# A bidirectional RWKV-7 time-mixing stage on one core: two interleaved chains become one, and the 64-row output products become 128-row products

## The chip, the core and the metric

The kernel runs on one core of a Trainium2 chip. The time is the device time of one execution in microseconds (us). The engines are TensorE (PE: matmuls and transposes), VectorE (DVE), ScalarE (ACT), GpSimd (POOL) and SyncE (SP, which here only issues DMAs). TensorE's results land in PSUM, 8 banks of 128 partitions by 512 floats; everything else on the chip lies in SBUF, 128 partitions wide.

## The reference

One layer over 2048 latent tokens and 256 context tokens, width 1024, all in float32: a modulated norm and one input projection feed two groups of heads (neighbourhood attention and RWKV-7 time mixing, 8 heads of 64 each), then come an output projection, a gated residual and a SwiGLU feed-forward block. The change lies in the time mixing, which runs a recurrence over a 64x64 state per head, once forward and once backward:

```python
def wkv_scan(s0, r, w, k, v, a, b, reverse):
    # S <- S diag(w) + (S a) b^T + v k^T ;  y = S r
    def step(s, inp):
        r_t, w_t, k_t, v_t, a_t, b_t = inp
        sa = jnp.einsum('bhvk,bhk->bhv', s, a_t)
        s = s * w_t[:, :, None, :] + sa[..., None] * b_t[:, :, None, :] + v_t[..., None] * k_t[:, :, None, :]
        return s, jnp.einsum('bhvk,bhk->bhv', s, r_t)
    ...
# per direction: the 256 context tokens from a zero state, then the 2048 latent tokens;
# y of both directions is summed, group-normed, a bonus added, multiplied by a gate g
mix = jnp.concatenate([o_na, o_rw], axis=-1) @ w_out
h = h + mod[2][:, None, :] * mix
h = h + mod[5][:, None, :] * swiglu(modulate(rms_norm(h, norm2_g), mod[3], mod[4]), ffn_w_in, ffn_w_out)
```

## The kernel before

There are three stretches. **Phase 1** (to about 900 us) makes the modulation, the norm and the input projection, and writes the operands of attention and time mixing to DRAM. **Phase 2** (about 900 to 1988 us) runs attention and time mixing together. **Phase 4** (from 1988 us) makes the output projection, the residual and the feed-forward block.

In phase 2 the recurrence is cut into 36 chunks of 64 tokens, numbered m = 2s + c (s from 0 to 17, c 0 or 1); both directions of a chunk are worked at once. The context takes s = 0 and 1, which give no output, so 32 chunks have outputs. Five kinds of work are prepared per chunk or per pair of s: `builds` (L1002: products of the decayed keys and queries, masked into `ga` and `gb` by DVE at L1014 and into `lx` by ACT at L1008), `inverses` (L1053 to L1113: the inverse of a triangular 64x64 block by 32x32 products, for both s of a pair), `lates` (L1035: transposes that give `tt`), and the loads of values into `zv` (`load_v`, L1126). The `ga` and `gb` live in a ring of NU = 17 units, in which unit (4s + head pair + SHIFT) mod NU is used.

The **chain** carries the state z from chunk to chunk. It runs as two streams, `chains(0)` and `chains(1)`, each with four of the eight heads (two pairs q, the two heads of a pair lying in partitions 0 to 63 and 64 to 127) and both directions dd. Per chunk and stream it is: copy z into the free half of `zv` (L1175 ACT, L1176 DVE); a batch of 8 products (L1180), copied by ACT to `rs` (L1184); a batch of 8 (L1188), copied back into `zv` by ACT and DVE (L1172); a batch of 8 (L1195), added to z by DVE (L1200); the output products, z by `ga` over 64 rows (L1206) and `zv` by `gb` over 128 rows (L1209), summed in PSUM; a multiplication of z by the chunk's decay (DVE, L1212); two ACT copies of the output (L1216) and four stores (`store_y`, L1134). Each float32 product shows as two MATMUL records in the trace, a transpose as one.

Who comes first is set by `emit` (L862): every stream of work yields what it will use and how long by a table, and the stream that could start earliest, shifted by its entry in `LATE`, is written next. The tile framework then orders instructions again by its own estimates while it resolves waits and buffers; `Run` and `issue_after` keep a batch in one piece in that second ordering. In phase 4 `TimeMixOutput` (TMO, L1239 to L1283) turns one tile of 128 tokens of y into the normed, gated mix: it loads `gup`, `lng` and `lnb` once (L1252) and `mx`, `y`, `v`, `gd` per tile (L1262 to L1265), multiplies by the gate's weights on PE (L1267), and runs some 14 operations on POOL, DVE and ACT, which form one chain for a tile. `prepared` transposes the mix on PE (L1404), and L1446 multiplies it by `w_out`; the first half of its sum is over attention, the second over time mixing. Phase 4's tiles reuse the SBUF of phase 2, so they wait for whatever lay at the same addresses.

Of the kernel before, what the change touches and what calls it, by code (L numbers as in the profile page):

```python
# [93 lines left out]
def phase1(k):  # L94

    tc, nc, I = k.tc, k.nc, k.I
    with ExitStack() as ctx:
# [295 lines left out]
        def work_build(ops, hp, t0):  # L393
# [4 lines left out]
            for dd in range(2):  # L398
# [19 lines left out]
                nc.gpsimd.tensor_copy(k.pc[:, s0:s0 + 2, hp // 2, :, 2 * dd + hp % 2],  # L418
# [428 lines left out]
NU = 17  # L847
# [10 lines left out]
LATE = (60, 60, 60, -10, -10, 0, 0, 0, 60, 0)  # L858
# [53 lines left out]
def phase2(k):  # L912
# [4 lines left out]
    with ExitStack() as ctx:  # L917
# [9 lines left out]
        pch = [ps[6 + g].tile([P, 2, 4, 64], F32, name=f"pch{g}") for g in range(2)]  # L927
# [43 lines left out]
        def build(s, hp, w):  # L971
# [164 lines left out]
        def chains(g):  # L1136

            z = ch.tile([P, 2, 2, 64], F32, tag=f"z{g}", name="z0", bufs=2)
            nc.gpsimd.memset(z, 0.0)
            if g:  # L1140
                load_v(0)
                yield "post", ("values", 0)
            yield "run", ("DMA", 2.2)
            for s in range(NS):
                yield "wait", ("inv", s // 2, 2 * g + 1)
                us = [U.pop((s, 2 * g + q)) for q in range(2)]
                for c in range(2):
                    m = 2 * s + c
                    yield "wait", ("values", m), ("late", m, g)
                    if g and m + 1 < 2 * NS:  # L1150
                        load_v(m + 1)
                        yield "post", ("values", m + 1)
# [4 lines left out]
        dq = [(dd, q) for dd in range(2) for q in range(2)]  # L1157
        kept = []

        def chain(s, c, g, z, us):  # L1160
            lx, j0 = LX[s // 2], 4 * (s % 2)
            zv = ZV[2 * s + c]
            tt = TT_.pop((2 * s + c, g))
            rp, up_ = pch[g][:, 0], pch[g][:, 1]
            gs = slice(P * g, P * g + P)

            def slot(h, dd, q):
                return zv[:, h, dd, P * g + 64 * q:P * g + 64 * q + 64]

            def keep():  # L1170
                for h, copy in ((0, nc.scalar.copy), (1, nc.vector.tensor_copy)):
                    copy(zv[H[h], h, :, gs], up_[H[h]].rearrange("p (d q) n -> p d (q n)", d=2))  # L1172

            yield "run", ("ACT", 0.27), ("DVE", 0.2)
            nc.scalar.activation(zv[H[0], 0, :, gs], z[H[0]].rearrange("p d q n -> p d (q n)"), AF.Copy)  # L1175
            nc.vector.tensor_copy(zv[H[1], 1, :, gs], z[H[1]].rearrange("p d q n -> p d (q n)"))  # L1176
            yield "run", ("PE", 0.57)
            for i, (dd, q) in enumerate(dq):
                for h in range(2):
                    nc.tensor.matmul(rp[H[h], i, :], us[q].ga[:, h, 2 * dd + c, :], slot(h, dd, q),  # L1180
                                     start=True, stop=True)
            yield "run", ("ACT", 0.27)
            rs = ch.tile([P, 4, 64], F32, tag=f"rs{g}", name="rs")
            nc.scalar.activation(rs, rp, AF.Copy)  # L1184
            yield "run", ("PE", 0.57)
            for i, (dd, q) in enumerate(dq):
                for h in range(2):
                    nc.tensor.matmul(up_[H[h], i, :], lx[H[h], 2 * g + q, j0 + 2 * dd + c, :], rs[H[h], i, :],  # L1188
                                     start=True, stop=True)
            yield "run", ("ACT", 0.27), ("DVE", 0.33)  # L1190
            keep()
            yield "run", ("PE", 0.57)
            for i, (dd, q) in enumerate(dq):
                for h in range(2):
                    nc.tensor.matmul(rp[H[h], i, :], tt[:, q, dd, H[h]], slot(h, dd, q),  # L1195
                                     start=True, stop=True)
            yield "run", ("DVE", 0.34)
            z2 = ch.tile([P, 2, 2, 64], F32, tag=f"z{g}", name="z2", bufs=2)
# [12 lines left out]
            yield "run", ("DVE", 0.34)  # L1211
# [484 lines left out]
```

## Time and profile before

| | |
|---|---|
| median of 3 runs | 3618.38 us (3614.16 to 3624.52) |
| the profiled execution | 3615.05 us, span 3613.3 us |
| mean granted TensorE clock | 0.944 of full speed |
| PE busy | 3433.7 us, 95% of the span |
| DVE, ACT, POOL busy | 68%, 43%, 29% |

A share of busy time is an average over phases with different limits; the stretches in the rows below are read one by one. The granted clock has two levels, 1.2 and 2.4 GHz; a stretch's value is the mean over it.

### The profile page before, as it was taken

How to read it: one execution, taken by the hardware profiler on the slowest of the kernel's cores; microseconds unless marked ns; L12 is line 12 of the kernel's file. 1: busy time of each engine (PE TensorE's matmuls, PEld its weight loads, DVE VectorE, ACT ScalarE, POOL GpSimd, SP SyncE). 2: the span in 40 equal slices, each digit the busy share in tenths (PEclk: the TensorE clock that was granted, in tenths of full speed). 3: DMA queues.
4: the chain of work that ended last, by engine and by line, in shares of the span. 5: the costliest groups of instructions: out<-in, count | busy, mean ns of one | idle time of the engine just before them, and what ended most of it. 6: DMA issues, size and time to landing. Idle time of an engine off the chain costs nothing. (4 is left out here: it accounts for less than half of the span.)

```text
span 3613.3 us, 66769 instructions
## 1 busy us (share of the span) xinstructions
PE 3433.7 (95%) x25202; PEld 2910.8 (81%) x25202; DVE 2469.6 (68%) x4570; ACT 1536.3 (43%) x3502; POOL 1056.3 (29%) x975
## 2 busy tenths in 40 slices
PE   7899999999889999999888999999899999899999
PEld 5787878889767677777676887888799999799998
DVE  7658786772675776667666674444877778777776
ACT  4524343442556566655433454323333334333332
POOL 3425543552000000000013243233433334433332
PEclk8999999999789899999866999999999999999999
DMA  7546666554544454444335455233422222412222
GB/s 238 158 146 201 188 185 190 166 165 123 160 121 129 117 145 140 124 132 123 93 91 154 141 193 170 94 96 102 140 65 70 71 70 72 162 62 71 71 70 68
DMA packets 461858, 458.52 MB, mean 127 GB/s; under 512 B 56656, under 2 KB 381664, under 8 KB 461536
## 3 DMA queue, kind: packets, MB, share of 16 engines
q1 hardware_dynamic: 461536, 454.25, 41.8%
q8 instruction: 199, 3.26, 0.4%
q14 instruction: 123, 1.01, 0.1%
HBM read 346.37 MB, written 107.75 MB: 126 GB/s over the span
## 5 line engine op out<-in xcount | busy, mean ns | idle before, releaser
L1317 ACT ACTIVATE w<-raw 128x512 fp32r<-128x512 f32 x440 | 270.4, 628 | 496.5 <-PE acc L1606 188.5
L1526 PE MATMUL acc<-ua,w 128*128 128x384 f32 x2464 | 469.1, 336 | 8.5 <-DVE h L1611 3.3
L1606 PE MATMUL acc<-w,fh 128*128 128x512 f32 x1408 | 437.5, 395 | 20.7 <-ACT fh L1317 8.4
L1318 DVE TENSOR_TENSOR w<-raw,w 128x512 fp32r<-128x512 f32 x308 | 280.5, 914 | 245.2 <-ACT w L1317 122.0
L1526 PEld LDWEIGHTS acc<-ua,w 128*128 128x128 f32 x2464 | 433.3, 189 | 11.8 <-DVE h L1611 3.7
L219 PE MATMUL acc<-u,wh 128*128 128x512 f32 (+3 forms) x1120 | 349.6, 392 | 11.7 <-ACT wh L209 5.6
L1606 PEld LDWEIGHTS acc<-w,fh 128*128 128x128 f32 x1408 | 267.2, 191 | 82.0 <-ACT fh L1317 10.2
L503 PE MATMUL acc<-wt,u 128*128 128x256 f32 x2496 | 320.8, 287 | 6.3 <-DVE sh L257 3.4
L503 PEld LDWEIGHTS acc<-wt,u 128*128 128x128 f32 x2496 | 307.4, 193 | 13.9 <-issue 5.5
L1597 POOL TENSOR_TENSOR raw<-raw,gate 128x512 f32<-128x512 f32 x132 | 179.6, 1370 | 415.7 <-DMA raw<-in_w_dram 356.2
L1606 PE MATMUL acc<-w,fl 128*128 128x512 f32 x704 | 270.5, 393 | 0.0
L1318 POOL TENSOR_TENSOR w<-raw,w 128x512 fp32r<-128x512 f32 x132 | 188.5, 1428 | 273.2 <-PE acc L1526 57.9
L219 PEld LDWEIGHTS acc<-u,wh 128*128 128x128 f32 (+1 forms) x1120 | 207.6, 193 | 58.1 <-issue 6.8
L1526 PE MATMUL acc<-ux,w 128*128 128x384 f32 x1232 | 252.0, 334 | 0.3 <-DVE w L1318 0.3
L1508 PE MATMUL acc<-ua,w 128*128 128x512 f32 x1056 | 241.7, 389 | 1.7 <-POOL w L1318 0.8
L1508 PEld LDWEIGHTS acc<-ua,w 128*128 128x128 f32 x1056 | 198.0, 188 | 43.4 <-POOL w L1318 1.3
L219 PE MATMUL acc<-u,wl 128*128 128x512 f32 (+3 forms) x560 | 218.4, 390 | 2.0 <-DVE wl L210 1.8
L1526 PEld LDWEIGHTS acc<-ux,w 128*128 128x128 f32 x1232 | 216.8, 188 | 1.6 <-DVE w L1318 1.3
L1002 PE MATMUL bank<-ga,bk 64*128 64x128 f32 (+1 forms) x1152 | 188.5, 314 | 8.4 <-DVE gb L1014 4.3
L1611 DVE TENSOR_TENSOR h<-h,acc 128x512 f32<-128x512 f32 x192 | 126.2, 683 | 101.3 <-PE acc L1606 101.0
L1002 PEld LDWEIGHTS bank<-ga,bk 64*128 64x128 f32 x1152 | 159.8, 213 | 30.0 <-issue 13.1
L1518 DVE TENSOR_TENSOR t<-acc,t 128x384 f32<-128x384 f32 x308 | 169.7, 551 | 13.9 <-PE acc L1526 7.3
(252 smaller groups left out, 6900.7 us busy)
## 6 DMA issues: line engine op xcount, KB each, us to landing
raw<-in_w_dram SPq DMA_DIRECT2D x132, 512.0 KB
raw<-in_w_dram SPq DMA_DIRECT2D x132, 256.0 KB
wada<-in_w_ada_dram SPq DMA_DIRECT2D x96, 256.0 KB
d_b<-bk SPq DMA_DIRECT2D x72, 256.0 KB
bkl<-d_b SPq DMA_DIRECT2D x144, 128.0 KB
bk<-d_b SPq DMA_DIRECT2D x72, 256.0 KB
d_b<-ar SPq DMA_DIRECT2D x136, 128.0 KB
xt<-in_x_dram SPq DMA_DIRECT2D x32, 512.0 KB
```

The lines of the kernel that those rows point to most:

```text
L219: nc.tensor.matmul(acc[:m, :n], a_[:, kk % 4, :m], b_[b][:, kk, :], start=(i == 0), stop=(i == 23))
L503: nc.tensor.matmul(acc[:, 256 * e:256 * e + 256], a_[b][:, kk, (j + e) * P:(j + e + 1) * P], ws[kk][:, h, :], start=(i == 0), stop=(i == 23))
L1002: nc.tensor.matmul(gp[:, j, 0:N], bk[H[h], j], u.ga[H[h], h:3:2 - h, j, :] if s > 1 else u.ga[H[h], h, j, :], start=True, stop=True)
L1317: nc.scalar.activation(hl[0], v, AF.Copy)
L1318: eng.tensor_tensor(hl[1], v, hl[0].bitcast(F32), op=sub)
L1508: nc.tensor.matmul(acc, hl[wi][:, kk, :], u[ui][:, 4 * hf + kk, :], start=q == 0, stop=q == 23)
L1518: vadd = lambda o, x, y: nc.vector.tensor_tensor(o, x, y, op=add)
L1526: nc.tensor.matmul(acc, w[wi][:, kk, :], u[i][ui][:, kk, :], start=q == 0, stop=q == 11)
L1597: nc.gpsimd.tensor_tensor(raw, raw, g2[:, o], op=ALU.mult)
L1606: nc.tensor.matmul(acc, a_[:, f, ts], w2[f][:, hl, :], start=(i == 0), stop=(i == 6 * np_ - 1))
L1611: nc.vector.tensor_tensor(hs[j][:, o], hs[j][:, o], acc, op=add)
```

## The change

The two streams become one, `chains()`, for all eight heads. Each batch is now 16 products instead of 8 (`rp` and `up` are whole PSUM banks), and the copies and DVE operations between the batches are twice as wide. `Run` keeps each batch in one piece. The output product z by `ga`, which had 64 rows, gets 128: `zp` holds z in one half of the partitions and zeros in the other, filled by two POOL copies per chunk. The ring has 16 units instead of 17, and waits that named a stream now name the whole chain. In the changed file the lines are L1181 (was L1180), L1191 (L1188), L1201 (L1195), L1214 and L1218 (L1206, L1209), L1175 (the new POOL copies), L1206 and L1221 (L1200, L1212), L1226 (L1216), L1260 (L1252), L1270 to L1273 (L1262 to L1265), L1275 (L1267), L1412 (L1404) and L1454 (L1446).

```diff
-NU = 17
+NU = 16
...
-LATE = (60, 60, 60, -10, -10, 0, 0, 0, 60, 0)
+LATE = (60, 60, -10, -10, 0, 0, 0, 60, 0)
...
-        pch = [ps[6 + g].tile([P, 2, 4, 64], F32, name=f"pch{g}") for g in range(2)]
+        rp, up_ = (ps[6 + i].tile([P, 8, 64], F32, name=n) for i, n in enumerate(("rp", "up")))
...
             if G > 1:
-                yield "wait", ("chain", 2 * G - 3, 0), ("chain", 2 * G - 3, 1)
+                yield "wait", ("chain", 2 * G - 3)
             if 4 * s + hp >= NU:
-                yield "wait", ("chain", (4 * s + hp - NU) // 4, (4 * s + hp - NU) % 4 // 2)
+                yield "wait", ("chain", (4 * s + hp - NU) // 4)
...
-                    yield "wait", ("chunk", m - 2, g)
+                    yield "wait", ("chunk", m - 2)
...
+        zp = ch.tile([P, 2, 2, 4, 64], F32, name="zp")
+        nc.gpsimd.memset(zp, 0.0)
+
+        def chains():
+
+            z = ch.tile([P, 2, 4, 64], F32, tag="z", name="z0", bufs=2)
...
-                yield "wait", ("inv", s // 2, 2 * g + 1)
-                us = [U.pop((s, 2 * g + q)) for q in range(2)]
+                yield "wait", ("inv", s // 2, 3)
+                us = [U.pop((s, hp)) for hp in range(4)]
                 for c in range(2):
                     m = 2 * s + c
-                    yield "wait", ("values", m), ("late", m, g)
-                    if g and m + 1 < 2 * NS:
+                    yield "wait", ("late", m, 0), ("late", m, 1)
+                    if m + 1 < 2 * NS:
...
-                    z = yield from chain(s, c, g, z, us)
-                    yield "post", ("chunk", m, g)
-                yield "post", ("chain", s, g)
...
+                    z = yield from chain(s, c, z, us)
+                    yield "post", ("chunk", m)
+                yield "post", ("chain", s)
+
+        dq = [(dd, q) for dd in range(2) for q in range(4)]
+
+        def chain(s, c, z, us):
...
-            rp, up_ = pch[g][:, 0], pch[g][:, 1]
-            gs = slice(P * g, P * g + P)
+            tt = [TT_.pop((2 * s + c, g)) for g in range(2)]
...
+                return zv[:, h, dd, 64 * q:64 * q + 64]
+
+            yield "run", ("ACT", 0.75), ("DVE", 0.65)
+            nc.scalar.activation(zv[H[0], 0], zf[H[0]], AF.Copy)
+            nc.vector.tensor_copy(zv[H[1], 1], zf[H[1]])
+            if s > 1:
+                for h in range(2):
+                    nc.gpsimd.tensor_copy(zp[H[h], h], z[H[h]])
+            yield "run", ("PE", 1.0)
+            run = Run(k)
             for i, (dd, q) in enumerate(dq):
                 for h in range(2):
-                    nc.tensor.matmul(rp[H[h], i, :], us[q].ga[:, h, 2 * dd + c, :], slot(h, dd, q),
-                                     start=True, stop=True)
-            yield "run", ("ACT", 0.27)
-            rs = ch.tile([P, 4, 64], F32, tag=f"rs{g}", name="rs")
+                    with run.next():
+                        run.last = nc.tensor.matmul(rp[H[h], i, :], us[q].ga[:, h, 2 * dd + c, :], slot(h, dd, q),
+                                                    start=True, stop=True).ins
+            yield "run", ("ACT", 0.6)
+            rs = ch.tile([P, 8, 64], F32, tag="rs", name="rs")
             nc.scalar.activation(rs, rp, AF.Copy)
-            yield "run", ("PE", 0.57)
+            yield "run", ("PE", 1.0)
...
-            yield "run", ("PE", 0.57)
+                    with run.next():
+                        run.last = nc.tensor.matmul(up_[H[h], i, :], lx[H[h], q, j0 + 2 * dd + c, :], rs[H[h], i, :],
+                                                    start=True, stop=True).ins
+            yield "run", ("ACT", 0.6), ("DVE", 0.6)
+            nc.scalar.copy(zv[H[0], 0], upf[H[0]])
+            nc.vector.tensor_copy(zv[H[1], 1], upf[H[1]])
+            yield "run", ("PE", 1.0)
...
-                yield "run", ("PE", -1.15)
+                yield "run", ("PE", -1.9)
+                run = Run(k)
                 for i, (dd, q) in enumerate(dq):
                     for h in range(2):
-                        nc.tensor.matmul(up_[H[h], i, :], us[q].ga[H[h], 2, 2 * dd + c, :], z[H[h], dd, q, :],
-                                         start=True, stop=False)
+                        with run.next():
+                            run.last = nc.tensor.matmul(up_[H[h], i, :], us[q].ga[:, 2, 2 * dd + c, :],
+                                                        zp[:, h, dd, q, :], start=True, stop=False).ins
                     for h in range(2):
-                        nc.tensor.matmul(up_[H[h], i, :], us[q].gb[:, h, 2 * dd + c, :], slot(h, dd, q),
-                                         start=False, stop=True)
-            yield "run", ("DVE", 0.34)
-            nc.vector.tensor_tensor(z2v, z2v, k.pc[:, s, g, c, :, None].to_broadcast([P, 4, 64]), op=ALU.mult)
+                        with run.next():
+                            run.last = nc.tensor.matmul(up_[H[h], i, :], us[q].gb[:, h, 2 * dd + c, :],
+                                                        slot(h, dd, q), start=False, stop=True).ins
...
-                yield "run", ("ACT", -0.54)
+                yield "run", ("ACT", -1.2)
                 for h in range(2):
-                    nc.scalar.copy(zv[H[h], h, :, gs], up_[H[h]].rearrange("p (d q) n -> p d (q n)", d=2))
-                kept.append(2 * s + c)
-                if kept.count(2 * s + c) == 2:
-                    store_y(2 * s + c)
+                    nc.scalar.copy(zv[H[h], h], upf[H[h]])
+                store_y(2 * s + c)
...
-        emit(banks, chains(0), inverses(), chains(1), lates(0), lates(1), builds(0), builds(1), at.products(), at.tiles(),
+        emit(banks, chains(), inverses(), lates(0), lates(1), builds(0), builds(1), at.products(), at.tiles(),
```

What the second ordering makes of it is seen on PE in the middle of phase 2. Before, one place with the outputs of a chunk and stream (`pch_9729`, `pch_9730` are the PSUM banks of the two streams):

```order
L1180 MATMUL pch_9730<-zv,ga_9773 64x64 x2
L1188 MATMUL pch_9730<-rs,lx 64x64 x8
L1206 MATMUL pch_9729<-z_20281,ga_9767 64x64 x2
L1209 MATMUL pch_9729<-zv,gb_9768 64x64 x2
L1206 MATMUL pch_9729<-z_20281,ga_9769 64x64 x2
L1209 MATMUL pch_9729<-zv,gb_9770 64x64 x2
L1206 MATMUL pch_9729<-z_20281,ga_9767 64x64 x2
L1209 MATMUL pch_9729<-zv,gb_9768 64x64 x2
L1206 MATMUL pch_9729<-z_20281,ga_9769 64x64 x2
L1209 MATMUL pch_9729<-zv,gb_9770 64x64 x2
L1195 MATMUL pch_9730<-zv,tt 64x64 x8
```

After, the outputs of a whole chunk begin so, and go on for 16 rows in this pattern:

```order
L1035 MATMUL bank_9724<-ident,bkl 128x128 x4
L1035 MATMUL bank_9725<-ident,bkl 128x128 x4
L1191 MATMUL up<-rs,lx 64x64 x16
L1201 MATMUL rp<-zv,tt 64x64 x16
L1214 MATMUL up<-zp,ga_9746 64x64 x2
L1218 MATMUL up<-zv,gb_9747 64x64 x2
L1214 MATMUL up<-zp,ga_9748 64x64 x2
L1218 MATMUL up<-zv,gb_9749 64x64 x2
L1214 MATMUL up<-zp,ga_9750 64x64 x2
```

The short batches and the short alternations of the two streams have gone; a batch of a chunk is followed by the next batch of the same chunk, with whatever other work is ready in between (here two sets of transposes between L1181 and L1191, nothing between L1191, L1201 and L1214).

The second place is the end of the chain on PE. Before, the last outputs are followed at once by phase 4's projection, whose first tiles had been transposed (L1404) and gated (L1267) among the last chunks:

```order
L1206 MATMUL pch_9730<-z_21040,ga_9753 64x64 x2
L1209 MATMUL pch_9730<-zv,gb_9754 64x64 x2
L1206 MATMUL pch_9730<-z_21040,ga_9755 64x64 x2
L1209 MATMUL pch_9730<-zv,gb_9756 64x64 x2
L1446 MATMUL acc<-wo_21259,mh 128x512 x2
L1446 MATMUL acc<-wo_21259,ml 128x512
L1446 MATMUL acc<-wo_21264,mh 128x512 x2
L1446 MATMUL acc<-wo_21264,ml 128x512
L1446 MATMUL acc<-wo_21269,mh 128x512 x2
L1446 MATMUL acc<-wo_21269,ml 128x512
```

After, the last outputs are followed by the transposes of the attention half, by 24 records of L1454 over that half (`wo_20929` to `wo_20944`), and among them the first gate product L1275:

```order
L1214 MATMUL up<-zp,ga_9760 64x64 x2
L1218 MATMUL up<-zv,gb_9761 64x64 x2
L1412 MATMUL mtp<-ident,mx 128x128 x4
L1454 MATMUL acc<-wo_20929,mh 128x512 x4
L1275 MATMUL g<-gup,gd 128x512
L1454 MATMUL acc<-wo_20929,ml 128x512
L1454 MATMUL acc<-wo_20934,mh 128x512 x2
L1454 MATMUL acc<-wo_20934,ml 128x512
L1454 MATMUL acc<-wo_20939,mh 128x512 x2
```

So no time-mixing tile is prepared before the chain's end; the sum's second half comes behind it.

The third place is SP's queue. Before, the loads of `gup`, `lng` and `lnb` stand ahead of loads of the transposes' input (`bkl`), several chunks before the end:

```order
L1126 DMA zv<-d_vs 64x256 x4
L1027 DMA bkl<-d_b 128x2x128 x2
L1252 DMA gup<-in_g_up_dram 128x4x64
L1252 DMA lng<-in_rows_dram 128x4x64
L1252 DMA lnb<-in_rows_dram 128x4x64
L1252 DMA gup<-in_g_up_dram 128x4x64
L1252 DMA lng<-in_rows_dram 128x4x64
L1252 DMA lnb<-in_rows_dram 128x4x64
L1027 DMA bkl<-d_b 128x2x128 x6
L1263 DMA y_21308<-d_y_82 128x512
L1264 DMA v<-d_vs 128x512
```

After, they stand among the stores of the last two chunks, and `mx`, `y`, `v` and `gd` behind the last store:

```order
L1260 DMA lnb<-in_rows_dram 128x4x64
L1260 DMA gup<-in_g_up_dram 128x4x64
L1134 DMA d_y_81<-zv 64x256
L1134 DMA d_y_82<-zv 64x256
L1134 DMA d_y_81<-zv 64x256
L1134 DMA d_y_82<-zv 64x256
L1260 DMA lng<-in_rows_dram 128x4x64
L1260 DMA lnb<-in_rows_dram 128x4x64
L1310 DMA gate_20973<-d_gate 128x1024
L1400 DMA mx<-d_mix 128x512
L1270 DMA mx<-d_y_81 128x512
L1271 DMA y_20978<-d_y_82 128x512
```

These loads write to addresses that the ring's last units held: with 16 units the units of s = 17 lie where phase 4 puts `gup`, `y`, `v` and `mx`.

## Rows read from the trace of the kernel before

**Rows 1.** The page's fourth part: the last chain by engine, share of the span.
```profile
PE 34%; DVE 2%; DMA 1%; issue 0%; POOL 0%; ACT 0%; DVEq 0%; SPq 0%; ACTq 0%
```

**Rows 2.** Stretches: from:to, length, busy of PE, PEld, DVE, ACT, POOL; PEclk, DMA, GB/s.
```profile
1041.00:1748.00 707.00, 675.52 (x8403) 516.78 (x8402) 482.28 (x1217) 422.39 (x1223) 17.82 (x17) 0.93 0.45 128
1748.00:1988.00 240.00, 203.48 (x2698) 160.77 (x2694) 161.42 (x282) 89.96 (x215) 43.67 (x30) 0.71 0.42 120
```

**Rows 3.** The same stretches, line L1206 alone: PE and PEld busy, clock.
```profile
1041.00:1748.00 707.00, 62.91 (x640) 37.18 (x640) 0.93 0.45 128
1748.00:1988.00 240.00, 39.54 (x384) 23.94 (x384) 0.71 0.42 120
```

**Rows 4.** The same stretches, line L1209 alone.
```profile
1041.00:1748.00 707.00, 63.08 (x640) 37.81 (x640) 0.93 0.45 128
1748.00:1988.00 240.00, 40.25 (x384) 24.34 (x384) 0.71 0.42 120
```

**Rows 5.** Timeline of PE: start, length, what; around 1851 us.
```profile
1849.27 0.68 PE L1188 MATMUL pch<-rs,lx 64*64 64x64 f32 x16
1849.88 1.16 PE L1002 MATMUL bank<-ga,bk 64*128 64x128 f32 x10
1850.97 0.33 PE L1206 MATMUL pch<-z,ga 64*64 64x64 f32 x4
1851.23 0.34 PE L1209 MATMUL pch<-zv,gb 128*64 128x64 f32 x4
...
1852.97 0.64 PE L1195 MATMUL pch<-zv,tt 128*64 128x64 f32 x16
1853.54 1.71 PE L1002 MATMUL bank<-ga,bk 64*128 64x128 f32 x16
```

**Rows 6.** Timeline of PE from 1804 us, another clock.
```profile
1804.02 0.48 PE L1206 MATMUL pch<-z,ga 64*64 64x64 f32 x4
1804.43 0.48 PE L1209 MATMUL pch<-zv,gb 128*64 128x64 f32 x4
...
1810.58 1.97 PE L1180 MATMUL pch<-zv,ga 128*64 128x64 f32 x32
```

**Rows 7.** Groups by line, PE, 1748 to 1988: xcount, busy, mean ns; idle before.
```profile
L1195 PE MATMUL pch<-zv,tt 128*64 128x64 f32 x382 | 21.4, 273 | 9.8 <-DVE zv L1172 9.6
...
L1267 PE MATMUL g<-gup,gd 128*128 128x512 f32 x12 | 10.0, 930 | 0.0
```

**Rows 8.** Groups by line and shape, DVE, 895 to 1985.
```profile
L1200 DVE TENSOR_TENSOR z<-pch,z 128x256 f32<-128x256 f32 x72 | 30.3, 421 | 26.2 <-PE pch L1195 25.5
...
L1283 DVE TENSOR_TENSOR mx<-mx,g 128x512 f32<-128x512 f32 x5 | 3.4, 683 | 4.3 <-PE g L1267 4.3
```

**Rows 9.** The same, ACT.
```profile
L1038 ACT ACTIVATE tt<-bank 128x512 f32<-128x512 f32 x72 | 42.7, 595 | 30.7 <-PE bank L1035 15.1 <-PE pch L1195 15.1
```

**Rows 10.** Groups by line and shape, POOL, whole span.
```profile
L339 POOL COPY sq<-rho 128x512 f32<-128x512 f32 x16 | 11.3, 707 | 0.6
```

**Rows 11.** Timeline of DVE, 1954 to 1971 us.
```profile
1954.53 0.29 DVE L1176 COPY zv<-z 64x256 f32<-64x256 f32 x1
...
1957.58 1.24 DVE L1176 COPY zv<-z 64x256 f32<-64x256 f32 x1
...
1969.65 0.68 DVE L1283 TENSOR_TENSOR mx<-mx,g 128x512 f32<-128x512 f32 x1
```

**Rows 12.** Timeline of POOL in the same stretch.
```profile
1956.61 2.07 POOL L1268 TENSOR_TENSOR mx<-mx,y 128x512 f32<-128x512 f32 x1 [10.82 <-DMA mx<-d_y]
```

**Rows 13.** Timeline of SP's queue: DMA issues.
```profile
1950.07 0.33 SPq L1262 DMA_DIRECT2D mx<-d_y  x1
...
1978.89 11.38 SPq L1134 DMA_DIRECT2D d_y<-zv  x8
```

**Rows 14.** Timeline of PE at the end of the chain.
```profile
1985.24 0.33 PE L1206 MATMUL pch<-z,ga 64*64 64x64 f32 x4 [0.53 <-DVE z L1200]
...
1988.32 1.22 PE L1446 MATMUL acc<-wo,mh 128*128 128x512 f32 x2 [0.90 <-ACT zv L1216]
```

More of the change, by code (lines that the diff above doesn't have):

```diff
@@ L417, in work_build @@
                 nc.scalar.activation(cum, cum, AF.Exp, scale=kappa)
-                nc.gpsimd.tensor_copy(k.pc[:, s0:s0 + 2, hp // 2, :, 2 * dd + hp % 2],
+                nc.gpsimd.tensor_copy(k.pc[:, s0:s0 + 2, :, dd, hp],
                                       pp[:, :, 64].rearrange("p (s c) -> p s c", c=2))
@@ L1134, in store_y @@
                     nc.sync.dma_start(out=k.d_y[dd][t0:t0 + 64, 256 * h:256 * h + 256], in_=zv[H[h], h, dd, :])
-        def chains(g):
-            z = ch.tile([P, 2, 2, 64], F32, tag=f"z{g}", name="z0", bufs=2)
+        zp = ch.tile([P, 2, 2, 4, 64], F32, name="zp")
+        nc.gpsimd.memset(zp, 0.0)
+        def chains():
+            z = ch.tile([P, 2, 4, 64], F32, tag="z", name="z0", bufs=2)
             nc.gpsimd.memset(z, 0.0)
-            if g:
-                load_v(0)
-                yield "post", ("values", 0)
+            load_v(0)
@@ L1170, in keep @@
[L1170 to L1176, printed above, removed]
-            yield "run", ("PE", 0.57)
+                return zv[:, h, dd, 64 * q:64 * q + 64]
@@ L1186, in chain @@
+            run = Run(k)
             for i, (dd, q) in enumerate(dq):
                 for h in range(2):
[L1188 to L1192, printed above, removed]
+                    with run.next():
+                        run.last = nc.tensor.matmul(up_[H[h], i, :], lx[H[h], q, j0 + 2 * dd + c, :], rs[H[h], i, :],
+                                                    start=True, stop=True).ins
@@ L1193, in chain @@
+            yield "run", ("ACT", 0.6), ("DVE", 0.6)
+            nc.scalar.copy(zv[H[0], 0], upf[H[0]])
+            nc.vector.tensor_copy(zv[H[1], 1], upf[H[1]])
+            yield "run", ("PE", 1.0)
+            run = Run(k)
             for i, (dd, q) in enumerate(dq):
                 for h in range(2):
-                    nc.tensor.matmul(rp[H[h], i, :], tt[:, q, dd, H[h]], slot(h, dd, q),
-                                     start=True, stop=True)
-            yield "run", ("DVE", 0.34)
@@ L1198, in chain @@
-            z2 = ch.tile([P, 2, 2, 64], F32, tag=f"z{g}", name="z2", bufs=2)
+                    with run.next():
+                        run.last = nc.tensor.matmul(rp[H[h], i, :], tt[q // 2][:, q % 2, dd, H[h]], slot(h, dd, q),
+                                                    start=True, stop=True).ins
+            yield "run", ("DVE", 0.65)
+            z2 = ch.tile([P, 2, 4, 64], F32, tag="z", name="z2", bufs=2)
             z2v = z2.rearrange("p d q n -> p (d q) n")
@@ L1201, in chain @@
             if s > 1:
-                yield "run", ("PE", -1.15)
+                yield "run", ("PE", -1.9)
+                run = Run(k)
                 for i, (dd, q) in enumerate(dq):
                     for h in range(2):
-                        nc.tensor.matmul(up_[H[h], i, :], us[q].ga[H[h], 2, 2 * dd + c, :], z[H[h], dd, q, :],
-                                         start=True, stop=False)
+                        with run.next():
+                            run.last = nc.tensor.matmul(up_[H[h], i, :], us[q].ga[:, 2, 2 * dd + c, :],
+                                                        zp[:, h, dd, q, :], start=True, stop=False).ins
                     for h in range(2):
-                        nc.tensor.matmul(up_[H[h], i, :], us[q].gb[:, h, 2 * dd + c, :], slot(h, dd, q),
-                                         start=False, stop=True)
-            yield "run", ("DVE", 0.34)
-            nc.vector.tensor_tensor(z2v, z2v, k.pc[:, s, g, c, :, None].to_broadcast([P, 4, 64]), op=ALU.mult)
+                        with run.next():
+                            run.last = nc.tensor.matmul(up_[H[h], i, :], us[q].gb[:, h, 2 * dd + c, :],
+                                                        slot(h, dd, q), start=False, stop=True).ins
+            yield "run", ("DVE", 0.65)
+            nc.vector.tensor_tensor(z2v, z2v, k.pc[:, s, c].rearrange("p d q -> p (d q)")[:, :, None].to_broadcast(
+                [P, 8, 64]), op=ALU.mult)
             if s > 1:
-                yield "run", ("ACT", -0.54)
+                yield "run", ("ACT", -1.2)
                 for h in range(2):
-                    nc.scalar.copy(zv[H[h], h, :, gs], up_[H[h]].rearrange("p (d q) n -> p d (q n)", d=2))
-                kept.append(2 * s + c)
-                if kept.count(2 * s + c) == 2:
-                    store_y(2 * s + c)
+                    nc.scalar.copy(zv[H[h], h], upf[H[h]])
+                store_y(2 * s + c)
             return z2
```

8 lines of the change are left out of this document (2 added, 6 removed).

## Prediction

> **What bounds the kernel now.** I read the page's chain first, then the stretches, then PE alone inside phase 2. The chain that ended last is PE, 34% of the span, and the rest of it is small [rows 1]; it covers only the last part of the program, so phase 2 has to be read by its own waits. The stretches split phase 2 in two. From 1041 to 1748 us, with attention still running, PE is busy 675.5 of 707 us (96%) at a granted clock of 0.93, while DVE has 482 and ACT 422 us [rows 2]: PE is the bound, and work taken from it is worth its time unless a new wait takes it back. From 1748 to 1988 us attention is over, PE is busy 203.5 of 240 us at a mean clock of 0.71 [rows 2]: a mixture of the two levels, so that every PE instruction costs more, and 36.5 us of waits in the recurrence, of which the third batch's wait for its copy alone is 9.6 us [rows 7]. Phase 4 follows without a gap: its first projection starts after 0.9 us of idle [rows 14].
>
> The sum is made against the profiled execution, 3615.05 us, which is 3.3 us (0.09%) under the median of three. Their spread is 10 us; a change under 0.3% (about 11 us) can't be told from none.
>
> **Term 1, the outputs on PE.** 640 records of L1206 and 640 of L1209 lie in the first stretch, 384 and 384 in the second [rows 3, 4]; at 64 records a chunk that is 20 and 12 chunks. At the upper clock four records of either line take 0.26 us from start to start, 65 ns each, since L1206 and L1209 have different tile forms and alternate; 16 records of one form in a row (L1195, 128*64) take 0.57 us, 36 ns each [rows 5]. After, both lines are 128*64. Per chunk: 16 groups of 0.26 are 4.2 us before, 64 records of 36 ns are 2.3 us after; I allow 40 ns, 2.6 us, since two operands alternate. That saves 1.6 us a chunk, 32 us over 20 chunks. At the lower clock a group takes 0.41 us, 6.6 us a chunk, and 32 records of one form took 1.97 us, 62 ns each, 3.9 us a chunk [rows 6]: 2.6 us saved. In the second stretch, mixed, I take 2.3 us, 28 us over 12 chunks.
>
> The Trainium skill speaks against the wider products: TensorEngine Tiling (Array Packing), section Overview, says that a contraction of 64 or less can be packed as two tiles for up to twice the throughput, which products padded to 128 rows give up. The trace differs: 16 records of the 64*64 form (L1188) take 0.61 us, 38 ns each, against 36 ns for the 128*64 form [rows 5]. By the page's factor the padded products would add up to a record's time for each pair, by the rows nothing; I go by the rows.
>
> **Term 2, half as many batches.** Two short batches with other forms between them become one. A change of form costs, by the same rows, 0.26 less four times 36 ns, 0.12 us. In PE's order the outputs' alternations go away (14 for each of 64 chunk-streams, less what other work had already split), and beside them roughly 100 other changes; 100 times 0.12 is 12 us, about 8 in the first stretch and 4 in the second.
>
> **What of it is kept in the first stretch.** 32 and 8 are 40 us freed on PE. Against it stands that one stream has four hand-offs per chunk that no second stream covers, with wider operations: 128x512 on DVE takes 683 ns where the 128x256 addition took 421 [rows 8], 128x512 on ACT 595 [rows 9]. The order shows attention, builds and transposes between most batches there, so they cover these; DVE and ACT do the same elements in fewer instructions. I keep three quarters, **-30 us**; bounds 0 (something else paces it, say the inverses on DVE) and -45 (all of it, and some waits too).
>
> **Term 3, the second stretch.** -28 for outputs and -4 for batches. The gate's products, 10.0 us of PE here [rows 7], and their transposes leave the stretch for phase 4: -13, which is paid below. The 9.6 us of the old wait and its smaller kin, some 17 us, go away with the second stream. New: in the order of the changed kernel the last chunks have nothing between their batches. A hand-off there is the operation (0.60 to 0.68 us by [rows 8, 9]) with a little around it; the one place where an addition of 0.42 us is waited for bare shows 0.53 us of idle [rows 14], so 0.8 us each now, four per chunk, 12 chunks: 38 us if all were bare; I take nine tenths, 34. Sum -28 - 4 - 13 - 17 + 34 = **-28 us**. Bounds: -45 (half of the hand-offs covered) and 0 (the clock stays at its lower level through the stretch because PE idles at each hand-off, so that outputs and batches save less than the hand-offs cost).
>
> **Term 4, phase 4's restart.** Before, tiles of TMO were ready when the last outputs ended. After, the loads of `gup`, `lng`, `lnb` wait for the last units' last readers and stand between the last stores, and `mx`, `y`, `v`, `gd` behind them. From the end E of the last output: copy and four stores with five loads on one queue, 3 to 5 us (eight stores of before took 11.4 us with their waits [rows 13], so this is the least); load issued at 1950.07, its reader starting at 1956.61: 6.5 us [rows 12, 13]; then TMO's chain for one tile, 1956.61 to the end of L1283 at 1970.33, 13.7 us [rows 11, 12]; transposes, split and its hand-offs some 2 us. The second half of the first sum starts at about E + 26. What PE does meanwhile of use is 24 products on attention: 1.22 us for two at the lower clock [rows 14], which counts some overlap, so I take 0.25 us each at the upper, 6 us, and the gate's products of the first tiles (some 3). Before, it started at E + 0.9. The loss is 26 - 1 - 6 + 5 for the gate products and transposes moved out of term 3 and not hidden = **+24 us**; bounds +13 (loads land in 2 us, TMO's operations run without rivals at 10) and +34 (second tile late as well).
>
> **Small edits.** 64 POOL copies of 64x512, 32 chunks by two; the nearest row, a POOL copy 128x512, takes 707 ns [rows 10], 45 us of POOL work beside 44 us that it has in the second stretch [rows 2]. Their reader L1214 comes three batches and three copies after z (over 5 us), so they are hidden; without that cover they would cost 0.7 to 1.4 us a chunk. They can also hold up DVE (below): I take **+3**, bounds 0 and +45. Ring of 16: a unit waits for the chain four s back, which `builds` already wait for by the inverse's turn: 0. `zp` shifts attention's first tiles by 1 KB onto phase 1's last: their loads start late by 2 us at most, **+1**. `LATE`, `pc`'s layout, `Run`: 0, same counts.
>
> Sum: 3615.05 - 30 - 28 + 24 + 3 + 1 = **3585 us**, 0.8% faster.
>
> **Rivals.**
> 1. *Phase 2's gain is kept whole, and the restart is short.* -40, -35, +13, +1: 3554 us. For it: PE at 96% in the first stretch. Against: the order's place of the loads. 0.15.
> 2. *The restart and the bare hand-offs eat it.* First stretch -18, second -8, restart +28: 3617 us, no change. For it: the empty order of the last chunks and a clock of 0.71. 0.17.
> 3. *POOL's copies hold DVE, slower.* A DVE copy of 64x256, 0.29 us at 1954.53, took 1.24 us at 1957.58 while a POOL addition ran from 1956.61 to 1958.68 [rows 11, 12]. The z copy and the zp copies start together on the same z in each chunk; if each zp copy stops DVE for its 0.7 us, that is 45 us, straight on the chain: 3615 - 58 + 24 + 1 + 45 = 3627 us. It decides from about 0.5 us a copy (33 us, what the other terms leave). Against: only the first of the two copies meets a DVE copy, and in the first stretch the chain has slack. 0.15. The Trainium skill has a rule of this kind: SBUF — State Buffer, section Who interferes with whom, says that DVE and GpSimd share a pair of ports, and that the one that comes second is blocked for the whole instruction when DVE's operation uses them; the trace's 1.24 us agrees with it.
> 4. *My forecast*, with the terms within their middle halves: 0.53.
>
> **Range and chances.** The forecast's own range is 3568 to 3604. Four parts in five need rival 2's middle and most of rival 1: 3553 to 3620 us. Faster by over 0.3% (under 3607): rival 1, the forecast and a little of the others, 0.69. Within: 0.17. Slower: rival 3 and the tail of rival 2, 0.14.
>
> **What would show it.** Right: L1214 and L1218 groups of four at 0.15 us; attention ending some 30 us earlier; the stretch from its end to the last output shorter by about 28 us; then a hole of some 20 us on PE around 24 products of L1454, ended by TMO. Wrong: the outputs still at 0.26 us (then terms 1 and 3 lose 60 us: slower), DVE copies L1172 near 1.2 us next to L1175 (rival 3), or PE idle at L1181 to L1214 in the first stretch (term 1's cover is missing). A restart without a hole would put the time near 3560 us.

## The result, and the profile after

The changed kernel took 3572.97 us (median of 4, 3558.60 to 3580.65) against 3617.47 us before: a ratio of 0.987, 95% interval 0.9835 to 0.9904. On another chip, beside two experiments, it took 3581.01 us (6 runs) against 3605.07 us: 0.9931, interval 0.9906 to 0.9955. The forecast was 3585 us, 0.8% faster; by these two measurements it is 1.3% and 0.7% faster.

Two of its executions were profiled, spans 3578.9 and 3579.7 us. Phase 2 falls into the same two stretches as [rows 2] when each is cut at the seventh inverse's last copy (before at 1747.4 us; after at 1714.4) and at the last output's end. Before, attention's last operation ends at 1752.0 us, close to that cut; after, it ends at 1675.9 us (second profile 1685.2), 38 us ahead of it. Stretches of the changed kernel, in the columns of [rows 2]:

```profile
1040.00:1714.00 674.00, 614.08 (x8429) 485.66 (x8430) 471.90 (x1124) 402.84 (x1112) 49.71 (x60) 0.95 0.47 134
1714.00:1930.00 216.00, 149.85 (x2670) 134.89 (x2668) 125.13 (x187) 74.97 (x149) 20.48 (x28) 0.70 0.33 94
```

and of its second profile:

```profile
1038.00:1724.00 686.00, 626.10 (x8433) 495.51 (x8433) 472.68 (x1124) 403.99 (x1112) 49.73 (x60) 0.93 0.47 132
1724.00:1932.00 208.00, 142.53 (x2660) 128.32 (x2661) 124.72 (x186) 75.00 (x148) 20.18 (x28) 0.72 0.35 98
```

The first stretch is 674 and 686 us where it was 707, the second 216 and 208 where it was 240. PE is busy 91% of the first stretch, no longer 96%. The outputs in the changed kernel's timeline of PE (the upper clock):

```profile
1927.76 0.22 PE L1214 MATMUL up<-zp,ga 128*64 128x64 f32 x1
...
1927.82 0.27 PE L1214 MATMUL up<-zp,ga 128*64 128x64 f32 x2
1927.88 0.22 PE L1218 MATMUL up<-zv,gb 128*64 128x64 f32 x1
...
1929.57 0.33 PE L1218 MATMUL up<-zv,gb 128*64 128x64 f32 x3
```

64 records from 1927.76 to 1929.9 us are 33 ns each; before, 65 [rows 5]. At the lower clock, in the same view around the first of them after attention:

```profile
1679.85 0.31 PE L1214 MATMUL up<-zp,ga 128*64 128x64 f32 x1
...
1683.48 0.66 PE L1035 MATMUL bank<-ident,bkl 128*128 128x128 f32 x4
```

that is 3.6 us for the 64, 57 ns each, where a chunk took 6.6 us [rows 6]. Then the restart, in the timeline of PE:

```profile
1941.61 1.09 PE L1412 MATMUL mtp<-ident,mx 128*128 128x128 f32 x4 [11.71 <-DMA mx<-d_mix]
1943.39 2.07 PE L1454 MATMUL acc<-wo,mh 128*128 128x512 f32 x4 [0.69 <-ACT mh L1325]
...
1952.51 0.39 PE L1454 MATMUL acc<-wo,ml 128*128 128x512 f32 x1
1955.24 1.12 PE L1275 MATMUL g<-gup,gd 128*128 128x512 f32 x2 [2.34 <-DVE mx L1291]
...
1958.20 1.88 PE L1275 MATMUL g<-gup,gd 128*128 128x512 f32 x2 [0.22 <-DVE mx L1291]
1959.28 1.72 PE L1454 MATMUL acc<-wo,mh 128*128 128x512 f32 x4
```

and in that of SP's queue:

```profile
1929.47 0.59 SPq L1260 DMA_DIRECT2D gup<-in_g_up_dram  x1
...
1932.01 2.49 SPq L1134 DMA_DIRECT2D d_y<-zv  x4
...
1936.53 0.42 SPq L1400 DMA_DIRECT2D mx<-d_mix  x1
```

SP's own waits from 1924 to 1945 us begin with

```profile
SPq L1260 <- PE up L1218: 4.4, 1, 4.4
```

The last output ends at 1929.9. PE waits 11.7 us for the attention half of `mx`, which is queued on SP behind `gup`, which waited for a reader of the ring's last units, and behind the stores; it does the 24 products on attention (1943.39 to 1952.9), waits again for TMO, and starts the second half at 1959.28, 29.4 us after the last output where [rows 14] have 0.9 us to the first product. From the last output to the end of the program it is 1649.0 us (second profile 1647.2), before 1625.9.

| part | forecast | first profile | second profile |
|---|---|---|---|
| first stretch (before 707) | -30 | -33 | -21 |
| second stretch (240) | -28 | -24 | -32 |
| last output to end (1625.9) | +24 | +23 | +21 |
| start, POOL | +4 | 0 | -2 |
| span (3613.3) | -30 | -34 | -34 |

### The profile page after: what moved, and what is told of

It is laid out like the page before. It is cut to its first block, busy times and chain, and to the rows that moved or that the text cites. A ratio compares the mean times of both kernels' runs of the same rounds, so it can differ in the third digit from the quotient of the medians.

```text
span 3578.9 us, 66596 instructions
## 1 busy us (share of the span) xinstructions
PE 3322.7 (93%) x25202; PEld 2855.9 (80%) x25202; DVE 2439.1 (68%) x4426; ACT 1506.5 (42%) x3330; POOL 1091.4 (30%) x1039
## 5 line engine op out<-in xcount | busy, mean ns | idle before, releaser
L1325 ACT ACTIVATE w<-raw 128x512 fp32r<-128x512 f32 x440 | 270.6, 627 | 498.8 <-PE acc L1614 181.3
L1175 POOL COPY zp<-z 64x512 f32<-64x512 f32 x64 | 45.5, 711 | 618.7 <-PE up L1214 505.4
```

The source lines that it names most:

```text
L1175: nc.gpsimd.tensor_copy(zp[H[h], h], z[H[h]])
L1325: nc.scalar.activation(hl[0], v, AF.Copy)
```

## The experiments

Each is cut like the table: first stretch, second stretch, rest, in us; ratios are to the kernel before on the same chip.

**The two halves of the change.** The output products alone (two streams, batches of 8, ring of 16 with its last units where they were):

```diff
+            if s > 1:
+                for h in range(2):
+                    nc.gpsimd.tensor_copy(zps[g][H[h], h], z[H[h]])
...
-                        nc.tensor.matmul(up_[H[h], i, :], us[q].ga[H[h], 2, 2 * dd + c, :], z[H[h], dd, q, :],
+                        nc.tensor.matmul(up_[H[h], i, :], us[q].ga[:, 2, 2 * dd + c, :], zps[g][:, h, dd, q, :],
```

> The kernel before with one part of the change alone: its output products of 64 rows become products of 128 rows with the zero-padded copy (one per stream, four POOL copies per chunk); two streams and batches of 8 stay. Ring of 16 units, its place chosen so that the last units lie where they lay before. Theory (most of the gain is the alternation of tile forms taken out of the outputs): first stretch 25 to 30 us shorter, the rest 10 to 20, total 3575 to 3585 us. Rival (the merged stream and its whole batches bring the gain): less than 12 us gained, over 3605 us.

And the merged stream alone, on the changed kernel with a ring of 17:

```diff
-                            run.last = nc.tensor.matmul(up_[H[h], i, :], us[q].ga[:, 2, 2 * dd + c, :],
-                                                        zp[:, h, dd, q, :], start=True, stop=False).ins
+                            run.last = nc.tensor.matmul(up_[H[h], i, :], us[q].ga[H[h], 2, 2 * dd + c, :],
+                                                        z[H[h], dd, q, :], start=True, stop=False).ins
```

> The changed kernel with its output products of z put back to 64 rows, straight from z, without the padded copy and its POOL copies, and with the ring of 17; the one stream and the batches of 16 stay. Theory (outputs bring the gain): the outputs cost 0.26 us a group again, some 60 us of PE over the 32 chunks, while the restart hole is gone with the old ring: 3600 to 3617 us. Rival (the single stream brings the gain): 3570 to 3585 us.

Measured: two_streams_128 3583.54 us, 0.9912 (0.9882 to 0.9943), as expected; one_stream_64 3625.12 us, 1.005 (1.0025 to 1.0075), 8 us above the range expected. Their stretches, first of two_streams_128, then of one_stream_64:

```profile
1046.00:1739.00 693.00, 642.37 (x8402) 499.06 (x8403) 484.17 (x1220) 420.70 (x1225) 59.11 (x102) 0.92 0.46 131
1739.00:1962.00 223.00, 163.35 (x2712) 139.78 (x2713) 161.64 (x283) 90.54 (x216) 60.34 (x72) 0.76 0.45 126
```

```profile
1034.00:1722.00 688.00, 647.14 (x8424) 504.19 (x8421) 467.37 (x1122) 406.04 (x1112) 18.08 (x18) 0.96 0.47 132
1722.00:1992.00 270.00, 211.34 (x2701) 169.17 (x2701) 154.87 (x235) 80.74 (x157) 42.92 (x30) 0.63 0.37 106
```

Nearly all of the gain comes with the output products; the merged stream alone is slower. The total of two_streams_128 is as expected, its parts are not: the first stretch is 14 us shorter (25 to 30 were expected, its clock is 0.92), the second 17. The merged stream isn't without effect: with it alone the first stretch is 19 us shorter than before (at a clock of 0.96, above the 0.93 of before, so that part of this can be the clock), the second 30 us longer, at a clock of 0.63. It also moves attention forward: it ends at 1685.3 us in one_stream_64, at 1744.5 in two_streams_128. In that second stretch the products are still the expensive alternation, and time-mixing tiles stand in PE's queue: the waits of PE in that stretch name their last operation on DVE,

```profile
PE mtp L1407 <- DVE mx L1286: 20.3, 2, 12.7
...
PE g L1270 <- DVE mx L1286: 6.1, 1, 6.1
```

The kernel of shift13 (next) ran on the same chip, and like these two and the kernel before it has no hole. The four compare the halves without the restart: the wider products bring 28 us with two streams (3611.34 to 3583.54) and 57 with one (3625.12 to 3567.86). Merging costs 14 us with the old products and gains 16 with the new, and that last step the intervals don't tell from nothing (0.9912 and 0.9879).

**The restart.** The ring's starting place moved, `SHIFT = 13` for `SHIFT = 1`:

> The changed kernel with the ring's starting place moved (SHIFT 13 instead of 1), so that the units of the last two chunks no longer lie where phase 4 loads gup, y, v and mx; nothing else differs. Theory (the restart is paid by the addresses of the ring's last units): the 29 us between the last output and the second half of the projection's first sum fall to under 3 us, and with 5 us of products already done in them the time falls by 18 to 23 us, from 3573 to about 3552 us. Rival (the hole is the latency of the time-mixing tiles themselves, which need the last chunks' stores wherever they are loaded): the hole stays over 20 us and the time within 8 us of 3573.

Measured: 3567.86 us, 0.9879 (0.9844 to 0.9915), and beside the changed kernel:

> The kernel of shift13 once more, beside the changed kernel. If closing the hole is worth what the two traces show from the sixth inverse's end to the end of the program (1967 against 1980 us): 9 to 16 us under changed_again. If that difference belongs to the one profile: within 6 us of it.

> The changed kernel itself, on the same chip and in the same rounds as the two others, to compare them with it: 0.985 to 0.990 of the kernel before.

3575.43 us, 0.9907 (0.9881 to 0.9933), against 3581.01 for the changed kernel, whose 0.9931 lies outside the 0.985 to 0.990 expected of it: 6 us apart, the intervals overlap. The hole is gone (first product 1.3 us after the last output, 1620.6 us to the end where the changed kernel has 1649.0; second profiles 1624.3 and 1647.2), so its cause is shown; yet its 23 to 28 us don't come back, and the 3552 us expected of shift13 was missed. The second stretch is 232 and 236 us instead of 216 and 208. The timeline of DVE of shift13 shows where a part of them goes:

```profile
1833.15 2.19 DVE L1053 STREAM_TRANSPOSE lu<-lx 128x1024 f32<-128x1024 f32 x1
...
1868.19 0.68 DVE L1289 TENSOR_TENSOR mx<-mx,lng 128x512 f32<-128x512 f32 x1
...
1869.39 0.40 DVE L1080 TENSOR_TENSOR lu<-lu,red 128x240 f32<-128x240 f32 x1
...
1870.31 0.68 DVE L1289 TENSOR_TENSOR mx<-mx,lng 128x512 f32<-128x512 f32 x1
1870.91 1.46 DVE L1076 TENSOR_TENSOR xtmp<-lu 128x768 f32<-128x768 f32 x1
...
1881.95 1.88 DVE L1085 STREAM_TRANSPOSE x1t<-lu 128x1024 f32<-128x1024 f32 x1
```

TMO's operations (`mx`) stand between those of the last inverse (`lu`, `xtmp`). From its first transposition to its last it takes 1833.15 to 1883.8, 50.7 us; in the changed kernel, where no tile is ready,

```profile
1835.88 2.15 DVE L1053 STREAM_TRANSPOSE lu<-lx 128x1024 f32<-128x1024 f32 x1
...
1872.25 1.88 DVE L1085 STREAM_TRANSPOSE x1t<-lu 128x1024 f32<-128x1024 f32 x1
```

38.2 us. The last four chunks wait for that inverse. So the next run put TMO behind it:

```diff
+                with tc.issue_after(k.last_inv) if j < 2 else nullcontext():
+                    tm.tile(mx[:, 512:1024], t)
```

> The kernel of shift13 with one more order on VectorE: the operations of the first two time-mixing tiles stand behind the last inverse instead of within it. Theory (shift13 lost most of the closed hole because those operations stretch the last inverse, 50.7 us from its first transposition to its last against 38.2 in the changed kernel): the last inverse takes 38 to 40 us again, the last output ends near 1932 us instead of 1943, and no hole follows; 3553 to 3560 us. Rival (then they delay the last four chunks by as much): last output at 1940 or later, 3565 us or more.

3573.01 us, 0.99 (0.9877 to 0.9923): the rival. The last inverse ends at 1886.6 instead of 1895.6 us, but the last four chunks take 57 us behind it instead of 47, with the last output at 1943.8. Counted from the seventh inverse's end, the second stretch is 226 us where shift13 has 232 and 236; the total doesn't show it. What TMO, the weights' splits and the chain need of DVE and ACT in the tail is paid in one place or another.

**The chunk before the last.** In the changed kernel it takes 23.5 us (DVE's L1221 ends at 1897.0 and 1920.4), the chunks beside it 8 and 9. The timeline of ACT in it:

```profile
1895.27 1.09 ACT L1038 ACTIVATE tt<-bank 128x512 f32<-128x512 f32 x2 [1.73 <-PE rp L1201]
1902.14 1.06 ACT L1325 ACTIVATE wo<-raw 128x1024 fp32r<-128x1024 f32 x1 [5.78 <-issue]
1903.10 0.61 ACT L1171 ACTIVATE zv<-z 64x512 f32<-64x512 f32 x1
1903.62 1.99 ACT L1325 ACTIVATE wo<-raw 128x1024 fp32r<-128x1024 f32 x2
1905.82 1.06 ACT L1325 ACTIVATE wo<-raw 128x1024 fp32r<-128x1024 f32 x1 [0.20 <-DMA raw<-in_w_out_dram]
1906.78 1.17 ACT L1226 COPY zv<-up 64x512 f32<-64x512 f32 x2
1909.45 1.06 ACT L1325 ACTIVATE wo<-raw 128x1024 fp32r<-128x1024 f32 x1 [1.50 <-DMA raw<-in_w_out_dram]
1911.79 1.06 ACT L1325 ACTIVATE wo<-raw 128x1024 fp32r<-128x1024 f32 x1 [1.29 <-DMA raw<-in_w_out_dram]
1912.87 0.60 ACT L1185 ACTIVATE rs<-rp 128x512 f32<-128x512 f32 x1
```

The splits of the output projection's weights (L1325) stand between the chain's copies (L1171, L1185). Three of them wait for their loads by the profile; the first waits 5.78 us with no releaser shown. The loads begin on SP's queue at 1897.78 us, behind those of `zv`; that the temporaries of the last inverse, which ended at 1882.9, hold them back by their addresses isn't shown. Two runs moved them. Earlier, by another buffer for six of the eight raw tiles (`wr5`, where attention lay):

> The changed kernel with the raw weights of the output projection (six of eight) loaded into a buffer where attention's tiles lay instead of into the place of the inverse's temporaries, so that they are split well before the last chunks. Theory (the chunk before the last takes 23.5 us instead of 8 to 9 because ScalarE waits for those weights between two of the chain's copies): that chunk takes 8 to 10 us, the last output ends 12 to 15 us earlier, 3558 to 3563 us. Rival (the splits cost the same wherever they stand, or the hole behind grows by it): within 6 us of 3573.

3585.23 us, 0.9933 (0.9909 to 0.9958): that chunk took 9.3 us, but a chunk behind attention's end and the last one became longer (46.8 and 16.1 us, before the edit 41.0 and 9.2), and the second stretch was 208 us, as in one of the changed kernel's own profiles. The ratio is that of changed_again: no gain, as the rival had it, though the time is 12 us above the 3573 that it named. Later, behind the chain's last operations, with the loads on ACT's queue:

```diff
+                with tc.issue_after(k.last_act), tc.issue_after(k.last_dve):
                     split((w[:, 0, :], w[:, 1, :]), raw, nc.vector)
```

> The changed kernel with the splits of the output projection's weights queued on ScalarE and VectorE behind the chain's last operations, that is in the hole before the restart, and their loads issued from ScalarE's queue. Theory (the chunk before the last lost 15 us to those splits, and the hole has room for them): that chunk takes 8 to 10 us instead of 23.5, the last output ends 12 to 15 us earlier, the hole keeps its length; from the sixth inverse's end to the end of the program 1965 to 1969 us instead of 1979.6, and the time 10 to 15 us under the changed kernel's. Rival (the splits are missed in the hole: the projection then waits for them): last output earlier, the hole longer by as much, no gain.

3575.06 us, 0.9907 (0.9882 to 0.9932), beside the changed kernel's 0.9931: the medians differ by 6 us, the intervals overlap. Its stretches:

```profile
1041.00:1726.00 685.00, 623.93 (x8425) 493.81 (x8422) 471.85 (x1123) 403.98 (x1112) 49.46 (x60) 0.93 0.47 132
1726.00:1917.00 191.00, 132.97 (x2670) 119.73 (x2668) 117.72 (x181) 69.19 (x143) 21.79 (x28) 0.78 0.32 90
```

The second stretch is 17 to 25 us shorter than the changed kernel's. The chunk before the last takes 15.4 us, not the 8 to 10 expected: 8 us of the difference. Another 11 us lie in a chunk around the eighth inverse that the edit doesn't touch: 28.5 us in both profiles of the changed kernel, 17.1 here, with the same order of work on PE. What differs is the clock: the granted one in it is 0.50 in both of those profiles and 1.00 here. The same 64 records, in the changed kernel and here:

```profile
1793.53 1.92 PE L1109 MATMUL bank<-lx,fs 32*32 32x32 f32 x64
```

```profile
1796.21 1.20 PE L1109 MATMUL bank<-lx,fs 32*32 32x32 f32 x64
```

The rest of the program is 8 to 10 us longer (1657.4 us), as the projection now waits longer; in the timeline of PE:

```profile
1931.47 1.09 PE L1413 MATMUL mtp<-ident,mx 128*128 128x128 f32 x4 [14.56 <-DMA mx<-d_mix]
...
1950.79 2.07 PE L1275 MATMUL g<-gup,gd 128*128 128x512 f32 x2 [9.28 <-DVE mx L1291]
...
1954.60 1.49 PE L1455 MATMUL acc<-wo,mh 128*128 128x512 f32 x4
```

From the last output (1916.9) to the second half it is 37.7 us instead of 29.4. So the hole takes back about what the chunk before the last gives, and the shorter second stretch is in large part the clock of one execution; whether the edit has a share in that clock isn't shown.

All three remedies together, with attention's buffers back at their old addresses:

> shift13, the order of tmo_after_inverse and the early weights together, and attention's buffers back at the addresses that they had before the change (a gap of 1 KB more). If the three costs are separate: last output near 1918 us, no hole, 3538 to 3545 us. If they hide each other: no better than the best of the three alone, about 3555 us.

3588.04 us, 0.9931 (0.9907 to 0.9954): second stretch 233 us. The sum is no better than the changed kernel, and 33 us above even the time expected if they hide each other; nor does it show what the addresses of attention's buffers cost.

**POOL's copies, and whole batches.** Each copy into `zp` made twice, and the batches without the order that keeps them in one piece (`run.next()` returns an empty context):

> The changed kernel with each POOL copy into the padded tile made twice (128 instead of 64, the same data). Theory (the copies are hidden and hold nobody up): VectorE's copies of z stay at 0.42 us, time within 6 us of 3573. Rival (each holds VectorE or the chain for its 0.6 us): 20 to 40 us slower, 3593 to 3613 us.

> The changed kernel without the order that keeps a batch in one piece; all else the same. Theory (whole batches save changes of tile form, priced at 0.12 us each, some 100 of them): 3575 to 3590 us. Rival (the second ordering leaves the batches nearly whole by itself): within 6 us of 3573.

3578.31 us, 0.9917 (0.9895 to 0.994), and 3577.78 us, 0.9904 (0.9873 to 0.9934): neither differs from the changed kernel's two ratios.

loose_batches is no test of whole batches. Its trace has the changed kernel's order of work on PE, DVE and ACT, and the same number of changes of tile form on PE: the second ordering leaves the batches whole by itself. It is in effect a third measurement of the changed kernel, 1.0% faster than before.

VectorE's copies beside POOL's, in the changed kernel (line, count: shortest, median, longest ns):

```profile
L1172 DVE COPY zv<-z x36: 424/424/818, 903.4 to 1920.5; 64x512 f32<-64x512 f32 x36
```

The median hides what POOL does, since 23 of the 36 copies don't meet a POOL copy at all (424 to 436 ns). Of the 13 that do, those that began first took 424 or 425 ns, and those that began while a POOL operation was running took 479 to 818 ns. One of either kind, first the line of DVE, then that of POOL:

```profile
1685.34 0.82 DVE L1172 COPY zv<-z 64x512 f32<-64x512 f32 x1
1684.60 1.28 POOL L1175 COPY zp<-z 64x512 f32<-64x512 f32 x2 [15.23 <-DVE z L1221]
```

```profile
1897.03 0.42 DVE L1172 COPY zv<-z 64x512 f32<-64x512 f32 x1
1897.24 1.35 POOL L1175 COPY zp<-z 64x512 f32<-64x512 f32 x2 [6.87 <-PE up L1214]
```

(The x2 are two POOL copies of about 0.61 us; in the first case the second of them begins at 1685.27.) So the copies do hold DVE, but seldom: over all DVE operations of phase 2 that meet one, the time beyond the median of their kind is 5.8 us, and 11.1 us with twice the copies. In the time of the kernel it doesn't show.

## Why the prediction was right, step by step

- **Term 1** (PE time of the outputs): the mechanism is shown by two_streams_128 and the 33 ns. The size: 2.1 us a chunk at the upper clock where 2.6 was allowed, 3.6 at the lower where 3.9 was. That the padding to 128 rows costs nothing on PE holds, and the page's factor for packed tiles (the Trainium skill, TensorEngine Tiling (Array Packing), Overview) doesn't show in these products of 64 columns.
- **Term 2** (12 us for fewer changes of form between batches): the count holds, the price is not shown. Counted over PE's records in order of start, the changes of form in phase 2 fall from 1341 to 797; 435 of those that went lay between outputs and belong to term 1, 109 elsewhere, where some 100 were forecast. No run prices these 109, since loose_batches has the same 797. The prediction's 14 alternations for each chunk and stream are 7 (eight groups of four records each); no term uses that number.
- **What is kept in the first stretch**: the step that was mis-sized. At an equal clock of 0.93 PE's busy time fell from 675.5 to 626.1 us, 49 us and not 40, and the stretch by 21: under half was kept, not three quarters. PE's idle time there rose from 31 to 60 us. PE idles 50.6 us in the first stretch of two_streams_128 too, so most of that comes with the cheaper products and not with the single stream. The waits in the changed kernel from 1041 to 1671 us are led by attention's softmax on ACT,

```profile
PE sw L793 <- ACT pr L784: 18.6, 19, 3.1
```

  which was 7.6 us before, up to 1747: 11 us of the 28. The rest is spread over many small waits and isn't assigned. That the -33 of the first profile came so near to -30 is luck of the clock (below). The sign "attention ending some 30 us earlier" was missed: it ends 76 and 67 us earlier, and only 8 in two_streams_128; it is the merged stream that lets attention run ahead of the inverses.
- **Term 3**: -28 against -24 and -32. That it came so near is partly luck: in the first profile PE's busy time fell by 54 us (45 forecast) and its waits grew by 30 (17 forecast), two errors of opposite sign. The bare hand-offs are there, but the longest wait of the stretch is for something that the prediction left out of the term: the last inverse. PE's waits from 1671 to 1935 us:

```profile
PE bank L1100 <- DVE x1t L1085: 26.2, 2, 25.0
...
PE up L1191 <- ACT rs L1185: 9.9, 5, 7.7
...
PE rp L1181 <- ACT zv L1171: 7.7, 3, 6.4
```

  25 us in one piece for the last inverse; the longest of the other two (7.7 and 6.4 us) are the weights' splits in the chunk before the last, and one of 8.0 us at L1201 falls into the eighth inverse, whose operations stand ahead of the chain's copy L1195 on DVE. Inverse and splits were in the trace of before, and neither had a term: there the last inverse took 54.9 us (1862.7 to 1917.6) with TMO in it, but PE had other work and waited 3.7 us for it.
- **Term 4**: +24 against +23 and +21, with E + 29.4 instead of E + 26 for the second half, and 24 products hidden in it. The place and the cause are shown by shift13. What the prediction did not see is that the hole isn't simply an extra cost that a better place would save: while no tile is ready, TMO leaves DVE free for the last inverse.
- **Rival 3** (POOL holds DVE): its price is shown wrong, its mechanism is there. Each of the 64 copies was to hold DVE for 0.7 us, 45 us in all; measured are 5.8 us over phase 2, because most DVE operations don't meet a copy or begin first, and pool_twice shows no cost in the time. Which of the two engines began first decides in all 13 cases above, as the rule on the shared ports has it (the Trainium skill, SBUF — State Buffer, Who interferes with whom).
- **Rival 1** needed the hole to be short: it was not. **Rival 2** needed the first stretch to keep -18 and the second -8: the first nearly came true at the lower clock, the second didn't.

Open: how the time between the seventh inverse and the last output would divide if the second ordering placed TMO, splits and inverse by their due times; each experiment moved a stall to another engine, and none was better than the changed kernel by more than can be measured.

## What to carry to other kernels

Small matmuls that alternate between tile forms took 1.7 to 2.0 times as long as products of one form; padding the smaller form with zeros, where partitions lie idle, took this away for the price of copies on an engine that was mostly idle. Time freed on the bound engine is kept only as long as what fills it is ready: here 21 of 49 us at an equal clock. And a hole found behind a changed address is worth closing only if the work that then moves forward has an engine to itself; look at who shares the in-order queue of the chain's last producer before counting the hole as gain.

## What the runs showed of the hardware

The granted clock of the same instructions differs from one execution to the next, and with it the time. The first stretch of kernels that do the same there took 674 us at a mean of 0.95 (changed kernel; shift13, 675), 682 at 0.94 (second profile of shift13; pool_twice, with more POOL copies), 682 to 686 at 0.93 (tmo_after_inverse, weights_in_hole, loose_batches, second profile of the changed kernel). That is 12 us between two profiles of one kernel on two chips, as much as a whole term of the forecast, and it is why stretches are compared at equal clock above where it can be done. On one chip the six executions of the changed kernel took from 3572.64 us at a mean of 0.95 to 3588.64 at 0.945 over the whole program. A single chunk with the same order of work took 28.5 or 17.1 us (weights_in_hole, above).
